# A two-group encoder layer on one core: other buffers for the first sweep's weights, another order of the output projection

## The chip, the cores and the metric

The kernel runs on one core of a Trainium2 chip. The metric is the device time of one execution in microseconds. The core has a TensorE (PE) for matrix products, a VectorE (DVE), a ScalarE (ACT) and a GpSimd (POOL) for elementwise work, and a SyncE (SP) whose queue issues nearly all DMA transfers of this kernel. Each engine takes its own instructions strictly in order; semaphores order them between engines.

## The reference

One encoder layer is applied with the same weights to two groups of tokens: a prompt of 1024 and a sample of 512, each with 16 meta tokens in front. In outline:

```
proj = rmsnorm(x) @ w_in            # 2048 -> 5440 columns, split into 8 parts
y_f   = real(fft2(u_f)) @ w_fmix    # Fourier mixing, 512 wide
y_mla = softmax attention, 8 heads  # low-rank queries, keys and values
y_d   = difference of two softmax attentions, 4 heads, relative bias
y = concat(y_f, y_mla, y_d) * silu(gate)
out = rmsnorm(x + y @ w_o)          # meta tokens dropped
```

All data are float32, and the result must be accurate to float32. Every matrix product is therefore three products of split operands: `hi*hi`, `hi*lo`, `lo*hi`, where `hi` is the rounded value in the PE's fast float32 form and `lo` is the remainder.

## The kernel before, in words

**Splitting.** `split` (lines 97 to 105) makes `hi` with one ACT instruction and `lo` with one DVE instruction that subtracts `hi` from the source. In the profile these are L101 and L102. A weight tile is 128 x 4 x 128 (256 KB); its halves are called `wh` and `wl` and lie in a pool `w` of three buffers, the raw tile `wr` in one of four.

**The weight stream.** `w_order` (line 197) writes down once the order in which all weight tiles are used. `fetch_w` (323) keeps up to three split tiles ready and up to three further entries loaded; `load_w` (272) issues the loads, `prepare_w` (292) splits. The program fixes the order of the PE's instructions alone. On ACT, DVE, POOL and SP the compiler's scheduler orders instructions beforehand, by its own estimate of when each becomes ready; at run time that order stands, also where a transfer takes longer than was estimated.

**Input projection.** `inproj` (378) uses one level of a Strassen-like scheme: the projection of pairs of weight column blocks with halves of the tokens becomes seven sweeps over sums and differences of operands, `b11`, `t1`, `t2`, `t3`, `t4`, `b21`, `b22`. There are 21 pairs in each (`PAIRS`). A sweep takes each pair in two weight entries ("jobs" below), each with 4 weight blocks x 3 products x 2 column ranges (512, and 256 or 264) = 24 matmuls (L374). The first three pairs of `b11` are treated together at the start; the other 18 give 36 jobs of the kind `a11`. Such a job loads two tiles, the block of the second column (`raws[0]`) and that of the first (`raws[1]`). The first is split for the PE. The difference of both, `ws` (one DVE subtraction, L302), goes to DRAM as `s3` (L306), for a later sweep. Both tiles come from one pool, `wq`, whose six buffers go to whichever load is next, as they come free. The loads are issued by line 247. A second's buffer is free after the subtraction, a first's only after its split, and that must wait until PE has released a `wh`/`wl` buffer. In the same sweep the next operand `t1` is built (L404, L430, L431, L102), results go to DRAM (L541 copies, L534 stores), and `bias_vectors` (1199) makes a small table through tiles of the tag `st`, four buffers, which nothing else uses in that sweep.

**Middle.** Up-projections (`upproj`), attention and Fourier mixing of the sample (G2), then of the prompt (G1). Attention has more work for ACT and DVE than for PE; `Chain.merge` therefore puts projection work between its steps, in units of a cost estimate (3 x 512 / 2400 = 0.64 for three 512-wide matmuls). `START[i]` is the amount of projection work put ahead of the first score product of stage i, so that its loads can land; stage 3 is the difference attention of G2. The score product is L1051; L1018 makes its key operand `kd`.

**Output projection.** The 16 row blocks of `y` are treated in four parts (`OUT_PARTS`, line 75), and a last piece (rows 12 to 15 of the prompt). `outproj_parts` (1263) runs beside the prompt's attention: for each of 16 column blocks `d`, the part's matmuls, then one addition per token block that takes the sum so far (`stage`, loaded by L1250 or L1244 or, in the first part, from the input by L1247) and the accumulator (L1295), and a store (L1301). All of these share six `stage` buffers. A sample part of 8 rows has 24 matmuls of 512 columns to an addition; a prompt part of 4 rows has 12, for each of two token blocks. The part that completes the sample also squares and scales (`outproj_scale`, L1256 to L1261). After that, `outproj_end` for G2 runs as a side generator, one step per `d` of the following parts: a load, a multiplication (L1356, on POOL for each third d, otherwise on DVE) and a store (L1357).

**Tail.** The last piece, rows 12 to 15 of the prompt's two token blocks, keeps all results in SBUF. `outproj` (1316) makes, for each d, 12 matmuls for a token block, the addition (L1338) and the squares and scales (L1259 to L1261). Before, the order is: both blocks for d 0 to 7 with the same weight tile; the first block for d 8 to 15, whose seven last tiles stay in an own pool `wt`; then the second block for d 8 to 15 in two column halves. `outproj_end` sums the squares over partitions (L114), takes the power -1/2 on POOL (L118), spreads it to rows (L129, L131) and multiplies 16 result tiles (L1360). The first block's end is advanced once per 0.7 units of the second block's first half:

```
            for gap in end:
                fill.some(0.7)
                if not fill.gens:
                    break
            fill.rest()
            fill = Chain(rows[2:3])
            fill.merge(weave(self.outproj_end(G1, 512, sums[1], sp, pa, (0, 256)), end, 1))
```

Of the kernel before, what the change touches and what calls it, by code (L numbers as in the profile page):

```python
# [74 lines left out]
OUT_PARTS = [(SAMPLE, 0, 8), (SAMPLE, 8, 8), (PROMPT, 0, 4), (PROMPT, 4, 8)]  # L75


class K:
    def __init__(self, tc, ins, outs):
        self.tc = tc  # L80
        self.nc = tc.nc
        self.ins = ins
        self.outs = outs
        self.scr = [{}, {}]
        self.uid = 0
        self.w_tail = 0, None
# [110 lines left out]
    def w_order(self):  # L197
# [43 lines left out]
        for _, e0, n in [*OUT_PARTS, (PROMPT, 12, 4)]:  # L241
            out += [("w", self.ins["wo"][b], k0, 4) for b in range(16) for k0 in range(e0, e0 + n, 4)]
        return out
# [19 lines left out]
    def split_w(self, i, wr, k0, n=4):  # L263
        left, pool = self.w_tail
        if len(self.w_list) - i > left:
            pool = self.wp
# [5 lines left out]
    def load_w(self):  # L272
# [17 lines left out]
        self.w_loaded.append((i, job, [self.raw_w(self.wq, "wq", *x) for x in src]))  # L290
# [908 lines left out]
    def bias_vectors(self, sp, pp):  # L1199
# [5 lines left out]
        def run():  # L1205
# [6 lines left out]
            for c in range(0, NDELTA, 516):  # L1212
# [3 lines left out]
                st = self.t(sp, [P, HALF], "st", bufs=4)[0:DIFF_H, 0:516]  # L1216
# [46 lines left out]
    def outproj_parts(self, yps, ys, sp, pp):  # L1263
# [3 lines left out]
        for ip, (blocks, e0, n) in enumerate(OUT_PARTS):  # L1267
# [14 lines left out]
            for i in range(0, len(todo), len(blocks)):  # L1282
# [24 lines left out]
                next(side, None)  # L1307
# [5 lines left out]
            if ip == 1:  # L1313
# [59 lines left out]
    def run_all(self):  # L1373
# [11 lines left out]
        with ExitStack() as es, ExitStack() as es2:  # L1385
# [14 lines left out]
            self.wq = p1.enter_context(pool("wq", 3, True))  # L1400
            slots = [p1.enter_context(pool("x0", 1, True))]
# [62 lines left out]
            with pool("d1", 2) as ap:  # L1464
                fill.merge(attend(G1, self.diff_ops, ap, 0))
            yf = es2.enter_context(pool("yf", 1))
# [7 lines left out]
            wt = es2.enter_context(pool("wt", 7))  # L1474
            ws = {}


            fill = Chain([self.outproj([(first, y0, sums[0]), (second, y1, sums[1])], range(8), (0, 512), ws, rp, sp, pa)])
            fill.rest()
            self.w_tail = (7, wt)  # L1480
            rows = [self.outproj([(p, y, a)], range(8, 16), cut, ws, rp, sp, pa)
                    for p, y, a, cut in ((first, y0, sums[0], (0, 512)), (second, y1, sums[1], (0, 256)),
                                         (second, y1, sums[1], (256, 256)))]
            Chain(rows[0:1]).rest()
            fill = Chain(rows[1:2])
            end = self.outproj_end(G1, 0, sums[0], sp, pa)
            for gap in end:
                fill.some(0.7)
                if not fill.gens:
                    break  # L1490
            fill.rest()
            fill = Chain(rows[2:3])
            fill.merge(weave(self.outproj_end(G1, 512, sums[1], sp, pa, (0, 256)), end, 1))
            fill.rest()
            drain(end)
# [165 lines left out]
```

## Time and profile before

| | |
|---|---|
| median of three runs | 2954.14 us (2951.81 to 2954.59) |
| the profiled execution's own time | 2959.01 us |
| its span, first to last instruction | 2957.2 us |
| PE busy | 2820.2 us, 95% |
| PE weight loads | 2470.0 us, 84% |
| DVE, ACT, POOL busy | 1776.5, 1148.7, 431.4 us |
| data moved by DMA | 566.51 MB, mean 192 GB/s |

PE is busy nearly everywhere; the busy share counts a matmul from its issue to its end, and matmuls overlap. So the number of matmuls in a stretch, beside the stretch's length, says more than the busy time: where matmuls have the same sizes, fewer of them in the same time are lost time. The granted clock (PEclk) says by how much PE's clock was cut; a cut clock does not show as idle time. A wait names the instruction that waited, what released it, the total, the count and the longest.

### The profile page before, as it was taken

Reading aid. Unit: us, or ns where it says so; the run is one execution under the profiler, and the core shown is the slowest. Engines: PE = TensorE matmul, PEld = TensorE weight load, DVE = VectorE, ACT = ScalarE, POOL = GpSimd, SP = SyncE. Lnnn points to the kernel's source line nnn. Section 1 sums busy time; section 2 is a strip of 40 time slices with the busy share of each in tenths; the row PEclk is TensorE's granted clock in tenths of the full one; section 3 lists DMA queues with packets and bytes.
Section 4 is the critical chain, followed back from the end, with each engine's and each line's share of the span. In section 5 each row is a group of like instructions: output and inputs, shape, how many; then the busy total and the mean of one; then the engine's idle time right before and its main releaser. Section 6 shows DMA issues by size and latency. Waiting matters only on the chain.

```text
span 2957.2 us, 45520 instructions
## 1 busy us (share of the span) xinstructions
PE 2820.2 (95%) x16360; PEld 2470.0 (84%) x16360; DVE 1776.5 (60%) x3263; ACT 1148.7 (39%) x2086; POOL 431.4 (15%) x536
## 2 busy tenths in 40 slices
PE   7889999999999999998899999999999989999986
PEld 6768888888888888886797888889999967888876
DVE  9236355476634445676856645566676649777656
ACT  5223221132322322224644743444555425444443
POOL 4010000011000100101211220222222212222100
PEclk9999999999999999999999999999999999999998
DMA  7668788888855656886555346544344476444254
GB/s 255 198 195 286 226 255 294 276 273 294 287 184 151 203 166 191 248 277 184 172 165 179 122 144 214 181 139 140 119 132 129 132 231 223 141 126 128 77 175 150
DMA packets 331379, 566.51 MB, mean 192 GB/s; under 512 B 50464, under 2 KB 121248, under 8 KB 330978
## 3 DMA queue, kind: packets, MB, share of 16 engines
q1 hardware_dynamic: 330704, 560.28, 59.4%
q0 software_dynamic: 448, 3.32, 0.5%
q8 instruction: 129, 2.11, 0.3%
q14 instruction: 98, 0.80, 0.1%
HBM read 388.39 MB, written 175.05 MB: 191 GB/s over the span
## 4 chain that ended last, share of the span: by engine, by line
PE 78%; DMA 9%; DVE 7%; issue 3%; ACT 2%; SPq 1%; POOL 1%; DVEq 0%; ACTq 0%; POOLq 0%
PE A L374 58%; PE S L962 6%; DMA wq<-in_win_dram 3%; PE T L1116 3%; PE S L1051 2%; PE T L1132 2%; PE T L1131 2%; PE T L1133 2%; DVE wl L102 1%; PE S L820 1%; DMA xr<-in_xt_dram 1%; DMA bt<-bvec 1%; DVE pe L904 1%; DVE ws L302 1%; DVE res L1360 1%
## 5 line engine op out<-in xcount | busy, mean ns | idle before, releaser
L374 PE MATMUL A<-x0h,wl 128*128 128x512 f32 x1376 | 358.4, 342 | 32.2 <-DVE wl L102 32.0
L101 ACT CAST wh<-wr 128x512 fp32r<-128x512 f32 (+1 forms) x342 | 206.2, 603 | 435.9 <-PE A L374 379.7
L374 PE MATMUL A<-x0h,wh 128*128 128x512 f32 x1376 | 359.3, 343 | 7.5 <-ACT x0h L104 7.5
L374 PE MATMUL A<-x0l,wh 128*128 128x512 f32 x1376 | 356.8, 341 | 0.1
L374 PE MATMUL A<-yh,wh 128*128 128x512 f32 (+1 forms) x800 | 328.7, 411 | 28.6 <-DVE stage L1295 19.1
L102 DVE TENSOR_TENSOR wl<-wr,wh 128x512 fp32r<-128x512 f32 (+1 forms) x342 | 245.2, 718 | 149.7 <-ACT wh L101 144.5
L374 PE MATMUL A<-yl,wh 128*128 128x512 f32 (+1 forms) x800 | 312.6, 391 | 1.6 <-DVE yl L102 1.5
L374 PE MATMUL A<-yh,wl 128*128 128x512 f32 (+1 forms) x800 | 312.1, 390 | 0.0
L374 PEld LDWEIGHTS A<-x0h,wl 128*128 128x128 f32 x1376 | 213.4, 190 | 68.4 <-DVE wl L102 38.5
L374 PE MATMUL A<-x1h,wh 128*128 128x512 f32 (+2 forms) x1040 | 269.0, 340 | 0.0
L374 PE MATMUL A<-x1l,wh 128*128 128x512 f32 (+2 forms) x1040 | 267.4, 338 | 0.0
L374 PE MATMUL A<-x1h,wl 128*128 128x512 f32 (+2 forms) x1040 | 266.7, 338 | 0.5 <-DVE wl L102 0.5
L374 PEld LDWEIGHTS A<-x0h,wh 128*128 128x128 f32 x1376 | 213.9, 191 | 39.1 <-ACT x0h L104 7.5
L374 PEld LDWEIGHTS A<-x0l,wh 128*128 128x128 f32 x1376 | 214.7, 190 | 31.4 <-DVE x0l L105 0.6
L101 ACT CAST wh<-ws 128x512 fp32r<-128x512 f32 x132 | 81.6, 620 | 357.6 <-PE A L374 301.4
L374 PEld LDWEIGHTS A<-yh,wh 128*128 128x128 f32 x800 | 154.9, 194 | 50.5 <-DVE stage L1295 15.1
L302 DVE TENSOR_TENSOR ws<-wq,wq 128x512 f32<-128x512 f32 x168 | 122.3, 728 | 115.8 <-DMA wq<-in_win_dram 94.0
L102 DVE TENSOR_TENSOR pl<-T,ph 126x512 fp32r<-126x512 f32 (+1 forms) x240 | 159.5, 685 | 45.3 <-ACT ph L101 43.7
L101 ACT CAST ph<-T 126x512 fp32r<-126x512 f32 (+1 forms) x240 | 132.6, 585 | 129.3 <-PE T L1116 126.6
L374 PEld LDWEIGHTS A<-yh,wl 128*128 128x128 f32 x800 | 154.1, 193 | 32.8
L374 PEld LDWEIGHTS A<-x1l,wh 128*128 128x128 f32 x1040 | 160.8, 189 | 23.1
L374 PEld LDWEIGHTS A<-x1h,wl 128*128 128x128 f32 x1040 | 159.5, 188 | 23.7 <-DVE wl L102 0.8
(211 smaller groups left out, 5712.7 us busy)
## 6 DMA issues: line engine op xcount, KB each, us to landing
wq<-in_win_dram SPq DMA_DIRECT2D x252, 256.0 KB, 4.4
wr<-in_wo_dram SPq DMA_DIRECT2D x128, 256.0 KB, 3.3
wr<-in_win_dram SPq DMA_DIRECT2D x98, 256.0 KB, 3.6
res<-stage SPq DMA_DIRECT2D x96, 256.0 KB, 3.0
stage<-res SPq DMA_DIRECT2D x88, 256.0 KB, 3.4
xr<-in_xt_dram SPq DMA_DIRECT2D x56, 388.0 KB, 5.5
stage<-y SPq DMA_DIRECT2D x48, 256.0 KB, 3.8
wr<-in_wuq_dram SPq DMA_DIRECT2D x48, 192.0 KB, 2.8
```

What stands on the lines that cost most here:

```text
L101: nc.scalar.copy(hi, src)
L102: nc.vector.tensor_tensor(lo, src, hi.bitcast(F32), ALU.subtract)
L302: nc.vector.tensor_tensor(sm, a, c, op)
L374: self.nc.tensor.matmul(ps, ww[:, kk, :], x[k][:, c:c + m], start=(k == 0 and ip == 0), stop=(k == nk - 1 and ip == 2))
L820: nc.tensor.matmul(o, z[:, c, :], tabs[j][:, c, hl, :], start=(c == chunks[0] and ip == 0), stop=(c == chunks[-1] and ip == 2))
L904: ttr(two(dst), src, two(add), 1.0, -3.0e38, ALU.add, ALU.max, accum_out=mx[0])
L962: nc.tensor.matmul(ps[:, c:c + n], qq, k[:, k0:k0 + n], start=(ip == 0), stop=(ip == 4))
L1051: nc.tensor.matmul(ps[:, c:c + n], qq[:, sub, sl], ks[sub][:, k0:k0 + n], start=(ip == 0), stop=(ip == 1))
L1116: nc.tensor.transpose(ps[0:g.kc, c, :], pn[0][:, a:a + g.kc], self.ident)
L1131: nc.tensor.matmul(o, vh[:, c, :], ph[:, c, :], start=(c == 0), stop=False)
L1132: nc.tensor.matmul(o, vh[:, c, :], pl[:, c, :], start=False, stop=False)
L1133: nc.tensor.matmul(o, vl[:, c, :], ph[:, c, :], start=False, stop=False)
```

## The change

It has three parts and a constant.

1. In `a11` jobs the second column's tile goes to a tile of the tag `st` of the pool `s1` (four buffers) in place of `wq`, so that the six buffers of `wq` serve the firsts alone. `bias_vectors` takes its tiles from the tag `u` (seven buffers) instead of `st`.
2. The second and third part of the output projection change places, so that the sample is completed in the third part. Its end runs beside the fourth part, with two steps in each of the first four d.
3. In the tail the first block takes all 16 d alone. The tiles of d 8 to 15 stay in a pool `wt` of eight buffers; those of d 0 to 7 are loaded and split a second time for the second block (eight more entries in the weight stream). The first block's end is advanced once per 1.7 units of the second block's first 8 rows and of the first column half of the others.
4. `START[3]` goes from 6.0 to 11.0.

```diff
-OUT_PARTS = [(SAMPLE, 0, 8), (SAMPLE, 8, 8), (PROMPT, 0, 4), (PROMPT, 4, 8)]
+OUT_PARTS = [(SAMPLE, 0, 8), (PROMPT, 0, 4), (SAMPLE, 8, 8), (PROMPT, 4, 8)]
...
+        out += [("w", self.ins["wo"][b], 12, 4) for b in range(8)]
...
-        left, pool = self.w_tail
-        if len(self.w_list) - i > left:
-            pool = self.wp
+        pool = self.w_kept if 8 < len(self.w_list) - i <= 16 else self.wp
...
-        self.w_loaded.append((i, job, [self.raw_w(self.wq, "wq", *x) for x in src]))
+        raws = [self.raw_w(self.wq, "wq", *x) for x in src[kind == "a11":]]
+        if kind == "a11":
+            raws.insert(0, self.t(self.w_side, [P, HALF], "st", bufs=4)[:, 0:512].rearrange("p (a b) -> p a b", a=4))
+            self.nc.sync.dma_start(raws[0], src[0][0][:, k0:k0 + 4, :])
+        self.w_loaded.append((i, job, raws))
...
-                st = self.t(sp, [P, HALF], "st", bufs=4)[0:DIFF_H, 0:516]
+                st = self.t(sp, [P, HALF], "u", bufs=7)[0:DIFF_H, 0:516]
...
-                next(side, None)
+                for _ in range(1 + (d < 4)):
+                    next(side, None)
...
-            if ip == 1:
+            if final:
                 side = self.outproj_end(G2, 0, (None, ssq), sp, pp)
...
+            self.w_side = s1
...
+            self.w_kept = es2.enter_context(pool("wt", 8))
...
-            wt = es2.enter_context(pool("wt", 7))
...
-            fill = Chain([self.outproj([(first, y0, sums[0]), (second, y1, sums[1])], range(8), (0, 512), ws, rp, sp, pa)])
-            fill.rest()
-            self.w_tail = (7, wt)
-            rows = [self.outproj([(p, y, a)], range(8, 16), cut, ws, rp, sp, pa)
-                    for p, y, a, cut in ((first, y0, sums[0], (0, 512)), (second, y1, sums[1], (0, 256)),
-                                         (second, y1, sums[1], (256, 256)))]
-            Chain(rows[0:1]).rest()
-            fill = Chain(rows[1:2])
+            Chain([self.outproj([(first, y0, sums[0])], range(16), (0, 512), ws, rp, sp, pa)]).rest()
+            for d in range(8):
+                del ws[d]
             end = self.outproj_end(G1, 0, sums[0], sp, pa)
-            for gap in end:
-                fill.some(0.7)
-                if not fill.gens:
-                    break
+            rows = [self.outproj([(second, y1, sums[1])], ds, cut, ws, rp, sp, pa)
+                    for ds, cut in ((range(8), (0, 512)), (range(8, 16), (0, 256)), (range(8, 16), (256, 256)))]
+            fill = Chain(rows[0:2])
+            for _ in end:
+                fill.some(1.7)
             fill.rest()
             fill = Chain(rows[2:3])
-            fill.merge(weave(self.outproj_end(G1, 512, sums[1], sp, pa, (0, 256)), end, 1))
+            fill.merge(self.outproj_end(G1, 512, sums[1], sp, pa, (0, 256)))
             fill.rest()
-            drain(end)
...
-START = (16.0, 15.6, 12.0, 6.0, 12.0, 8.4)
+START = (16.0, 15.6, 12.0, 11.0, 12.0, 8.4)
```

More of the change, by code (lines that the diff above doesn't have):

```diff
@@ L85, in __init__ @@
         self.uid = 0
-        self.w_tail = 0, None
     def nm(self, s):
```

## The prediction

> **What bounds the kernel now.** I read the page first, for the engine shares and the slices.
>
> ```profile
> span 2957.2 us, 45520 instructions
> ...
> PE   7889999999999999998899999999999989999986
> ...
> PEclk9999999999999999999999999999999999999998
> ```
>
> A slice is 74 us. PE is the bound; it is short of work in the first three slices, in two in the middle (near 1350), in one near 2400, and at the end. These are the places of the change. Next the windows, which give a stretch its length, the busy time and count of PE, PEld, DVE, ACT and POOL, then the granted clock, the DMA share and GB/s.
>
> ```profile
> 84.00:240.00 156.00, 131.72 (x686) 108.57 (x685) 49.63 (x64) 35.64 (x72) 12.56 (x6) 0.96 0.61 191
> 240.00:360.00 120.00, 119.48 (x678) 104.34 (x677) 59.60 (x80) 33.46 (x63) 4.32 (x2) 1.00 0.82 264
> 2040.00:2280.00 240.00, 240.00 (x1514) 219.86 (x1513) 159.87 (x341) 128.43 (x232) 64.78 (x88) 1.00 0.41 129
> 2395.00:2460.00 65.00, 49.50 (x217) 40.20 (x216) 40.71 (x77) 22.55 (x38) 9.49 (x11) 0.89 0.87 269
> 2460.00:2814.00 354.00, 336.99 (x1934) 290.05 (x1934) 262.24 (x589) 162.91 (x298) 75.47 (x106) 1.00 0.43 137
> 2834.00:2900.00 66.00, 65.58 (x283) 52.75 (x282) 38.20 (x59) 37.96 (x59) 0.00 (x0) 1.00 0.46 145
> 2900.00:2944.00 44.00, 31.77 (x218) 30.41 (x216) 30.03 (x69) 17.32 (x37) 1.96 (x2) 0.84 0.53 180
> ```
>
> 84 to 240 us is most of the first sweep, 240 to 360 the next, with the same kind of matmuls. The second row runs 678 in 120 us, 0.177 us each. At that rate the first sweep's 686 would take 121.4 us; they took 156. So 34.6 us are lost there: 24.3 idle by the waits below, most of the rest at a cut clock (0.96). The waits of that stretch say on what, the first two lines for PE and DVE, the others for SP's own queue:
>
> ```profile
> DVE ws L302 <- DMA wq<-in_win_dram: 90.9, 22, 6.7
> ...
> PE A L374 <- DVE wl L102: 24.3, 14, 3.8
> ```
>
> ```profile
> SPq L247 <- DVE ws L302: 83.4, 27, 5.3
> ...
> SPq L247 <- DVE wl L102: 7.7, 7, 2.9
> ```
>
> PE waits for a weight's low part on DVE. DVE does that late because its queue has the subtraction `ws` of a later job ahead of it, and that waits for a load. The load was issued late because SP waited for a buffer that an earlier subtraction frees (83.4 us), seldom for one that a split frees (7.7 us). The chain of work shows one turn of this circle, start and duration:
>
> ```profile
> 129.04 0.70 DVE ws L302
> ...
> 129.76 0.33 SPq L247
> ...
> 131.13 5.72 DMA wq<-in_win_dram
> ...
> 136.97 0.70 DVE ws L302
> 137.69 3.15 DMA wq<-in_win_dram
> ...
> 140.92 0.70 DVE ws L302
> ```
>
> Two jobs take 140.92 - 129.04 = 11.88 us, and two transfers lie in line. PE needs 48 x 0.177 = 8.5 us for two jobs. So the circle is the bound of this sweep, not DMA's rate: the next sweep moves 264 GB/s with PE at full rate.
>
> **Part 1, own buffers.** The load at 137.69 starts 0.02 us after the subtraction at 136.97 ends, whose buffer it takes. With four buffers for the seconds, such a load is free of that subtraction and goes out a job or more earlier; the firsts, alone in six buffers, can run up to six jobs ahead of the split. Without the 3.15 us the circle is 8.7 us for two jobs, against PE's 8.5. 686 matmuls are 14.3 such pairs, so 3 us of the 34.6 would remain, a gain of 32. That is one bound. The other comes from what stays: a first's buffer still comes free only after a split, and the scheduler may now put one subtraction between each two splits. Then each job has an issue, a landing, a subtraction and a split in line.
>
> ```profile
> L102 DVE TENSOR_TENSOR wl<-wq,wh 128x512 fp32r<-128x512 f32 x26 | 21.1, 831 | 3.2 <-ACT wh L101 3.2
> ```
>
> With this row's 0.83 us that is 0.33 + landing + 0.70 + 0.83. At a landing of 3.15 us a job takes 5.0 us, at 5.72 us it takes 7.6, against 5.94 now; over the 26 splits of the row that is from -24 to +43 us. The same bytes in less time (191 x 156 / 125 = 238 GB/s) lie between the two window rows. I take -20: nearer to the first bound, since SP's wait for subtractions is eleven times that for splits, but not all of it, since landings will differ from the scheduler's estimate as they do now. The Trainium skill, page "DMA: Bandwidth & Descriptors", section "Latency and other measured facts", speaks against earlier loads: an HBM access takes 0.2 us on average but 2 us at high load, so an estimate by it, 3.15 + 1.8 us to land, would make a job 6.8 us and the sweep 23 us slower. This trace agrees as far as the two landings above go, 3.15 us alone and 5.72 us among others.
>
> The table's tiles in "u" instead of "st" cost nothing: four more tiles pass through seven buffers of which each unit of the sweep takes one. If that cover is gone, a result copy waits for one such transfer once or twice, under 5 us, which is inside the bounds.
>
> **Part 2, order of the parts.** The stage 2395 to 2460 is the passage from one attention to the next. PE has 15.5 idle us there, and DMA is at 0.87, its highest. What moves there, with count and KB, and what PE waits for:
>
> ```profile
> stage<-in_xt_dram SPq DMA_DIRECT2D x12, 256.0 KB, 3.6
> res<-stage SPq DMA_DIRECT2D x12, 256.0 KB, 4.7
> ...
> stage<-res SPq DMA_DIRECT2D x6, 256.0 KB, 5.7
> wr<-in_wo_dram SPq DMA_DIRECT2D x6, 256.0 KB, 4.7
> out_dram<-stage SPq DMA_DIRECT2D x6, 256.0 KB, 4.2
> ```
>
> ```profile
> PE A L374 <- DVE stage L1295: 11.8, 3, 7.0
> ```
>
> These are the prompt's four-row part, with an addition to each 12 matmuls, and the end of G2 beside it. After the change the sample's second half runs here: for the same 144 matmuls 6 loads and 6 stores of sums instead of 24 in all, 12 weights instead of 6, no end of G2 (12 transfers). That is 42 transfers becoming 24, 4.7 MB less, and at 269 GB/s 17.5 us of DMA time; additions that need a `stage` buffer fall from 12 to 6. Against this stand two ACT and one DVE instruction more per d for the sample's squares and scales, off PE's path as long as PE waits for additions. The bounds are -20 (15.5 idle and 5 of the clock, 49.5 x 0.11) and, if squares and scales delay the attention's own steps, +5. I take -10, half of the idle and clock loss, since the attention's loads stay.
>
> What moves out goes to two places. The prompt's four-row part now lies in 2040 to 2280, where PE has 240 of 240 us and DMA 0.41: 16 additions, 32 sums moved and 16 weights fewer are 16 transfers more, 4.2 MB in 240 us; I cost them at nothing, the cover being the attention's gaps, which PE fills; without it each exposed landing is some 4 us. The end of G2 goes into 2460 to 2814.
>
> ```profile
> L1356 DVE TENSOR_TENSOR stage<-stage,rb x11: 678/686/691, 2340.9 to 2537.3; 128x512 f32<-128x512 f32 x11
> ...
> L1356 POOL TENSOR_TENSOR stage<-stage,rb x5: 1281/1299/1681, 2374.5 to 2519.1; 128x512 f32<-128x512 f32 x5
> ```
>
> There DVE is busy 262 of 354 us and PE already idles 17. Eleven multiplications of 0.69 us on DVE and five of 1.30 us on POOL, 14 us of work, lie beside the score chain on the same engines, and each may stand ahead of a step of it while its load lands. Some 4 of the 16 are there already (they end at 2537). So 0 to +10; I take +3. The Trainium skill, page "SBUF — State Buffer", section "Who interferes with whom", says that a DVE instruction with two SBUF inputs contends with a GpSimd instruction that reads SBUF; by it the five on POOL would also hold up DVE, for at most 6.5 us, which the range has.
>
> **The constant.** At the start of stage 3 PE waited once for the first score's keys:
>
> ```profile
> PE S L1051 <- DVE kd L1018: 5.2, 1, 5.2
> ```
>
> Five more units are 5 / 0.64 = 7.8 groups of three 512-wide matmuls. A matmul of that size is 66 / 283 = 0.233 us by the windows row from 2834, so 5.5 us of work cover that wait, if its weights are there: three entries are split ahead, and 7.8 groups need 2.6. It goes from -5 to, if they aren't, 0 (the work is only done earlier). I take -3.
>
> **Part 3, the tail.** What PE waits for from 2814 on, and three of DVE's groups from 2834 on:
>
> ```profile
> PE A L374 <- DVE res L1338: 9.4, 3, 6.3
> ...
> PE T L114 <- DVE ssq L1260: 2.6, 2, 1.4
> PE T L129 <- POOL rc L118: 1.6, 2, 1.1
> ```
>
> ```profile
> L1338 DVE TENSOR_TENSOR res<-stage,A 128x512 f32<-128x512 f32 x24 | 16.5, 686 | 14.6 <-PE A L374 14.6
> L1260 DVE TENSOR_TENSOR ssq<-ssq,tmp 128x512 f32<-128x512 f32 x22 | 15.2, 692 | 9.5 <-ACT tmp L1259 9.1
> ...
> L1360 DVE TENSOR_TENSOR res<-res,rb 128x512 f32<-128x512 f32 x16 | 9.8, 688 | 1.0 <-ACT rb L131 1.0
> ...
> L102 DVE TENSOR_TENSOR wl<-wr,wh 128x512 fp32r<-128x512 f32 x14 | 9.6, 689 | 4.9 <-ACT wh L101 4.9
> ```
>
> From 2900 to 2944 the first block's 16 multiplications stand in DVE's queue ahead of the second block's additions, and PE, out of accumulators, waits 9.4 us; its sum over partitions and rows wait some 2 more (half of 2.6 and 1.6; the other half belongs to the last end, which stays). Afterwards 16 rows of the second block lie beside that end. The clock of 0.84 there costs some 5 us more (31.77 x 0.16). So up to -16. What is added: eight weights, each 256 KB, an ACT cast and a DVE split. PE's work is the same. In the second block's first 8 rows a row is 12 x 0.233 = 2.8 us of PE, and DVE has a split, an addition, a square's sum and 2.56 / 1.7 = 1.5 multiplications, 4.5 x 0.69 = 3.1 us. DVE falls 2.4 us behind there, and may wait for a weight besides. The first block's 16 rows need 3 x 0.69 = 2.1 of 2.8 us. If the order is as unlucky as now, the saved 11 us come back as waits of rows. Bounds -16 and +4; I take -9.
>
> **The sum** for the profiled execution: -20 - 10 + 3 - 3 - 9 = -39 us. It took 2959.0 us, 2957.2 of it span, and the median of the runs is 2954.1; I take the difference from the median: **2915 us**.
>
> **The rivals.** All of the sweep's loss goes: -32 to -36 in place of -20, the sum 2902. For it: 8.7 us against 8.5. Against it: the circle has other queues in it, the stores in SP's.
>
> The sweep gains nothing, since firsts now wait for splits as the seconds did for subtractions: the rest alone, -19, gives 2935. This happens where a landing in the one-for-one order is about 4.1 us (0.33 + 4.1 + 0.70 + 0.83 = 5.94); it is also what follows if the scheduler leaves the loads where they were, that is, if the change does not do what it says.
>
> Slower: the same one-for-one circle with landings above 4.1 us. At 5.72 us it costs 26 x 1.64 = +43 us; with the other -19 the time is 2978. It outweighs the rest from a landing of 4.8 us on (26 x 0.73 = 19). For it: five of six buffers held by firsts that wait for a split is what a longer lead leads to. Against it: a transfer alone in line landed in 3.15 us, and the seconds no longer share those buffers.
>
> **How the numbers follow.** Forecast 0.42, full gain 0.24, no gain in the sweep 0.21, slower 0.13. The range is 2892 to 2950: below it lies full gain with the better bounds of passage and tail (some 0.08), above it most of the slower case (0.12). A measurement of this kernel can tell about 0.2% (6 us) from no change. Faster by more than that: the first three cases but for a tenth of the third and some of the mishaps in the passage and the tail, 0.80; within it 0.07; slower 0.13.
>
> **What would show it.** Right: from 84 us on, matmuls at 0.177 us each, PE's wait for the low part under 10 us, SP's wait for subtractions under 20, the sweep over about 20 us sooner; in the passage after the prompt's first attention PE idle near 8 us and DMA below 0.75; PE's wait for L1338 under 4 us; the multiplications L1360 apart from each other. Wrong: a circle in the chain of work with a load, a subtraction and a split per job; PE waits for L1051 in the last attention growing by over 6 us; a DVE without a gap in the second block's rows with PE waiting for it.

## The result, and the profile after

| | before | after |
|---|---|---|
| median of four runs | 2954.07 us (2951.81 to 2954.59) | 2913.76 us (2912.1 to 2918.23) |
| the profiled execution | 2959.01 us | 2912.1 us |
| its span | 2957.2 us | 2910.2 us |

The ratio after to before is 0.9867, with an interval of 0.9850 to 0.9884: 1.33% or 40.3 us faster, by medians. The two profiled executions differ by 46.9 us, since that of before lies 4.9 us above its median and that of after 1.7 us below. Terms read from the traces therefore add up to more than the medians show.

In the kernel after, lines stand a few further down: the split is L100 and L101 (L101 and L102 before), the load of a second tile L292, the subtraction L305, the matmul L377, the score product L1054, the addition of a part's sum L1298, the sum of squares L1263, the residual addition L1342, the end's multiplication L1364. The page of after, in the lines shown of before:

```profile
span 2910.2 us, 45585 instructions
...
PE   8999999999999999999999999999999989999986
```

Two of the three thin slices at the start are full now, and so are the two in the middle; the passage's slice and the end show as they did. The stages, as windows (length, then busy time and count of PE, PEld, DVE, ACT, POOL, then granted clock, DMA share, GB/s): the first sweep, the difference attention of G2 up to the prompt's MLA attention, its first part alone, and the passage from the prompt's first attention to its second.

```profile
84.00:240.00 156.00, 149.11 (x819) 125.22 (x818) 65.39 (x79) 44.92 (x87) 15.59 (x8) 0.99 0.69 221
1289.10:1905.00 615.90, 592.91 (x3602) 520.05 (x3601) 385.62 (x848) 319.19 (x666) 99.12 (x181) 0.99 0.56 173
1289.10:1439.30 150.20, 139.07 (x803) 119.71 (x802) 111.65 (x232) 85.16 (x180) 19.97 (x37) 0.95 0.60 187
2350.00:2437.20 87.20, 78.65 (x402) 66.39 (x401) 66.85 (x137) 49.64 (x89) 15.42 (x17) 0.96 0.64 195
```

In the first sweep 819 matmuls run in the 156 us that held 686. At the prediction's 0.177 us each they need 145.0 us, so 11.0 us of loss are left of 34.6. By count, a job of 24 matmuls takes 156 x 24 / 819 = 4.6 us on average, against 156 x 24 / 686 = 5.5 before. The last three windows are cut at the same matmuls as these of before:

```profile
1311.80:1938.90 627.10, 597.56 (x3601) 524.71 (x3601) 388.90 (x850) 319.23 (x666) 98.05 (x181) 0.98 0.55 171
1311.80:1472.40 160.60, 141.21 (x802) 121.19 (x802) 119.78 (x245) 87.10 (x185) 22.52 (x39) 0.94 0.58 179
2384.20:2480.90 96.70, 80.55 (x403) 67.44 (x402) 65.77 (x130) 35.71 (x63) 17.18 (x20) 0.93 0.81 255
```

The stretch of 3601 matmuls lost 11.2 us in length and the passage 9.5. What PE waits for in the whole run of after:

```profile
PE S L1054 <- DVE sd L909: 16.3, 14, 6.5
PE A L377 <- DVE wl L101: 8.7, 8, 2.6
PE A L377 <- DVE res L1342: 7.8, 3, 4.2
PE A L377 <- DVE stage L1298: 7.7, 1, 7.7
```

The low part's wait was 24.3 us in 14 places of the first sweep alone (84 to 240 us); there it is now:

```profile
PE A L377 <- DVE wl L101: 5.3, 5, 2.6
```

Of the wait for the addition of a part's sum, the three places of the passage (11.8 us) are gone. The wait for the residual addition, which part 3 was about, went only from 9.4 to 7.8.

Every one of these kernels has 16360 matmuls, so the k-th starts earlier or later by a number that adds up, stage by stage, what was gained so far. In us against the profile of before, for the kernel after and for the four parts alone (experiments below; between places where an experiment runs the code of before, its figures still move by up to 5 us, the difference of one execution from another):

| up to matmul | start before | after | part 1 | constant | part 2 | part 3 |
|---|---|---|---|---|---|---|
| 1200, end of the first sweep | 267.3 | -22.4 | -22.7 | -3.3 | -0.2 | -1.6 |
| 7200, G2's difference attention begins | 1311.8 | -22.6 | -23.0 | -3.6 | +0.1 | -1.9 |
| 11200, the prompt's MLA attention runs | 2004.8 | -35.0 | -25.4 | -14.2 | -1.4 | -6.5 |
| 13600, the passage begins | 2384.2 | -34.2 | -25.4 | -14.2 | -0.1 | -6.5 |
| 14000, its end | 2480.9 | -43.7 | -24.9 | -15.0 | -8.6 | -8.5 |
| 15600, end of the last attention near | 2775.9 | -42.5 | -24.9 | -14.8 | -4.0 | -7.8 |
| 16359, the last | 2945.5 | -47.4 | -26.0 | -15.5 | -5.5 | -12.3 |

### The profile page after: what moved, and what is told of

The parts are those of the page before. It is cut to its first block, busy times and chain, and to the rows that moved or that the text cites. A ratio compares the mean times of both kernels' runs of the same rounds, so it can differ in the third digit from the quotient of the medians.

```text
span 2910.2 us, 45585 instructions
## 1 busy us (share of the span) xinstructions
PE 2807.3 (96%) x16360; PEld 2458.4 (84%) x16360; DVE 1774.6 (61%) x3271; ACT 1152.5 (40%) x2094; POOL 431.7 (15%) x536
## 4 chain that ended last, share of the span: by engine, by line
PE 74%; DMA 7%; DVE 6%; ACT 2%; issue 2%; SPq 1%; POOL 1%; DVEq 0%; ACTq 0%; POOLq 0%
PE A L377 56%; PE S L965 6%; PE T L1119 3%; PE T L1134 2%; PE T L1135 2%; PE T L1136 2%; PE S L1054 2%; DMA raw<-kd 1%; DVE pe L907 1%; DVE wl L101 1%; DVE pe L1069 1%; PE S L823 1%; DMA wr<-in_wo_dram 1%; DMA stage<-res 1%; DMA stage<-y 1%
## 5 line engine op out<-in xcount | busy, mean ns | idle before, releaser
L100 ACT CAST wh<-wr 128x512 fp32r<-128x512 f32 (+1 forms) x350 | 210.9, 603 | 427.3 <-PE A L377 366.6
L377 PE MATMUL A<-x0h,wh 128*128 128x512 f32 x1376 | 358.5, 342 | 9.6 <-ACT x0h L103 7.5
L377 PE MATMUL A<-x0h,wl 128*128 128x512 f32 x1376 | 355.5, 340 | 8.9 <-DVE wl L101 8.7
L377 PE MATMUL A<-x0l,wh 128*128 128x512 f32 x1376 | 355.9, 340 | 3.4 <-DVE x0l L104 3.4
L377 PE MATMUL A<-yh,wh 128*128 128x512 f32 (+1 forms) x800 | 326.0, 408 | 16.0 <-DVE res L1342 7.8
L101 DVE TENSOR_TENSOR wl<-wr,wh 128x512 fp32r<-128x512 f32 (+1 forms) x350 | 252.7, 723 | 134.2 <-ACT wh L100 130.1
L377 PE MATMUL A<-yl,wh 128*128 128x512 f32 (+1 forms) x800 | 310.1, 388 | 0.0
L377 PE MATMUL A<-yh,wl 128*128 128x512 f32 (+1 forms) x800 | 310.1, 388 | 0.0
L377 PE MATMUL A<-x1h,wh 128*128 128x512 f32 (+2 forms) x1040 | 268.7, 339 | 0.0
L377 PE MATMUL A<-x1l,wh 128*128 128x512 f32 (+2 forms) x1040 | 267.1, 338 | 0.0
L377 PE MATMUL A<-x1h,wl 128*128 128x512 f32 (+2 forms) x1040 | 266.3, 337 | 0.0
L377 PEld LDWEIGHTS A<-x0h,wl 128*128 128x128 f32 x1376 | 212.6, 189 | 42.6 <-DVE wl L101 12.4
L377 PEld LDWEIGHTS A<-x0h,wh 128*128 128x128 f32 x1376 | 212.7, 189 | 41.6 <-ACT x0h L103 7.5
L377 PEld LDWEIGHTS A<-x0l,wh 128*128 128x128 f32 x1376 | 214.1, 190 | 35.3 <-DVE x0l L104 4.3
L100 ACT CAST wh<-ws 128x512 fp32r<-128x512 f32 x132 | 81.7, 620 | 363.3 <-PE A L377 306.7
L101 DVE TENSOR_TENSOR pl<-T,ph 126x512 fp32r<-126x512 f32 (+1 forms) x240 | 159.4, 685 | 43.9 <-ACT ph L100 42.8
L377 PEld LDWEIGHTS A<-yh,wh 128*128 128x128 f32 x800 | 152.4, 191 | 37.1 <-DVE stage L1298 8.1
L100 ACT CAST ph<-T 126x512 fp32r<-126x512 f32 (+1 forms) x240 | 132.6, 586 | 128.3 <-PE T L1119 125.7
L377 PEld LDWEIGHTS A<-x1l,wh 128*128 128x128 f32 x1040 | 160.7, 188 | 23.3
L377 PEld LDWEIGHTS A<-yh,wl 128*128 128x128 f32 x800 | 151.8, 190 | 33.0
L377 PEld LDWEIGHTS A<-x1h,wl 128*128 128x128 f32 x1040 | 159.5, 188 | 23.0
L377 PEld LDWEIGHTS A<-x1h,wh 128*128 128x128 f32 x1040 | 159.5, 188 | 22.2
```

What stands on the lines that cost most here:

```text
L100: nc.scalar.copy(hi, src)
L101: nc.vector.tensor_tensor(lo, src, hi.bitcast(F32), ALU.subtract)
L377: self.nc.tensor.matmul(ps, ww[:, kk, :], x[k][:, c:c + m], start=(k == 0 and ip == 0), stop=(k == nk - 1 and ip == 2))
```

## The experiments

### Each part alone

**Part 1 alone.** The hunks of `load_w` and `bias_vectors` and the line that sets `w_side` go into the kernel before.

> The kernel before with part 1 alone (own buffers for the seconds, the table's tiles in the other tag). Theory (a circle of loads and subtractions bounds the first sweep, and the second transfer in line is what goes): PE is ahead by 22 us after the first sweep, as in the trace of after, all later stages as before, the time about 2932 us. Rival (the sweep's gain needs the rest of the change, or the scheduler's other order of later stages takes part of it back): 2940 us or more, or later stages that differ from before by over 5 us.

Measured: 2928.99 us, ratio 0.9926 (0.9914 to 0.9939), 22.5 us less than the 2951.53 of the kernel before beside it. In its trace 819 matmuls lie between 84 and 240 us, as many as in the kernel after; it is 22.7 us ahead at the end of the sweep, and from there on the table moves by under 5 us. The theory holds.

**The constant alone.** `START[3]` goes from 6.0 to 11.0 in the kernel before.

> The kernel before with START[3] = 11 alone. The prediction gave it -3 us; the trace of after is ahead by 10 to 12 us more between 1340 and 1890 us. Theory A (the constant does all of that, by giving the loads of the whole stage more time, not the first wait alone): about -10 us, 2944. Theory B (the constant is worth the first wait, the remainder is a chance of the new order on ACT, DVE and SP that part 1 or 2 brings): -3 to -5 us, 2950.

Measured: 2943.57 us, ratio 0.9977 (0.9967 to 0.9986), 8.0 us less (4.1 to 9.7). That is theory A's number, with an interval that reaches theory B's. In the table its gain lies where the constant acts, 10.6 us between matmuls 7200 and 11200; but 8.9 of them come by matmul 8000, in the stage's first part, so it isn't the loads of the whole stage that gain, as theory A has it. What PE waits for at the start of that stage, before (1311.8 to 1475 us) and with the constant (1308 to 1465):

```profile
PE T L891 <- DVE pl L102: 5.9, 3, 3.1
PE S L1051 <- DVE kd L1018: 5.2, 1, 5.2
PE S L1051 <- DVE sd L904: 4.9, 5, 3.0
```

```profile
PE S L1051 <- DVE sd L904: 6.5, 6, 2.6
PE T L1116 <- DVE pe L1066: 3.5, 2, 1.8
PE A L374 <- ACT wh L101: 3.5, 1, 3.5
...
PE A L374 <- DVE wl L102: 0.3, 1, 0.3
```

The keys' wait of 5.2 us goes, and 3.8 us of waits for weights (the last two lines) take its place, the case in which the projection work put ahead runs out of split weights. But three waits for `pl` (the low part of the transposed probabilities), 5.9 us, go as well. The granted clock in this window is 0.98, against 0.94 in that of before:

```profile
1308.30:1462.00 153.70, 138.74 (x817) 119.77 (x815) 114.73 (x238) 86.15 (x182) 19.87 (x37) 0.98 0.58 185
```

In the kernel after the wait for the keys is gone too and that for `pl` is down to 0.6 us, yet the clock of its window is 0.95. So what the clock adds to the constant's gain isn't settled by these traces.

**Part 2 alone.** The line of `OUT_PARTS` and the two hunks that advance and start the sample's end go into the kernel before.

> The kernel before with part 2 alone (order of the output projection's parts, the end of the sample in the fourth part). Theory (the passage near 2400 us is short of stage buffers and DMA): -10 us in the passage, +2 in the last attention, 2946 us in all, the passage's DMA share under 0.8. Rival (the passage's loss is that of the attention's own loads): under 4 us of gain, 2950 or more.

Measured: 2947.66 us, ratio 0.9988 (0.9979 to 0.9997). By the table 8.5 us are gained in the passage and 4.6 given back in the last attention, and the passage's DMA share is 0.63: the theory's picture, with a time between its number and the rival's. In the passage the only long wait left is the first score product of the next attention:

```profile
PE S L1051 <- DVE sd L906: 8.4, 1, 8.4
```

**Part 3 alone.** The eight more weight entries, the pool `wt` of eight and the new order of the tail go into the kernel before.

> The kernel before with part 3 alone (first block first, eight weights a second time, the end at 1.7 units a step). Theory (11 us of waits go, half of it comes back as DVE falling behind in the second block's rows): -5 us, 2949, with PE's waits for L1338 and its like spread over several rows. Rival (the gain is whole, the trace of after fell short by chance): -9 us or better, 2945.

Measured: 2948.22 us, ratio 0.9991 (0.9982 to 1.0), 3.3 us less, at the edge of what can be told. By the table it gains 4.5 us behind matmul 15600, the kernel after 4.9. PE's wait for the residual addition is 8.6 us in 4 places, one of them 4.2 us long, against 9.4 in 3 before: the theory's number holds, but the waits aren't spread over several rows.

The four single gains are 22.5 + 8.0 + 3.9 + 3.3 = 37.7 us, and the whole change has 40.3 against the 2954.07 beside it, or 37.8 against the 2951.53 of the single parts. So the parts add up within the intervals; none needs another.

### What in part 1 does it

**The ten buffers shared by job.** The four new buffers take both tiles of every other job (those with odd `q`) and the six take both tiles of the rest:

```diff
+        if kind == "a11" and q == 1:
+            raws = [self.t(self.w_side, [P, HALF], "st", bufs=4)[:, 0:512].rearrange("p (a b) -> p a b", a=4) for _ in src]
...
```

> The kernel before with the same four further buffers for the first sweep's loads (and the 0/1 table moved as in the change), but parted by job and not by kind: every other job takes both of its tiles from the four, the jobs between take both from the six. A load then waits for a job 4 or 6 before it, where it waited for one 3 before it; in the change every first waits for a split 6 before it and every second for a subtraction 4 before it. Theory, how many jobs fit into the buffers is what counts: 2928 to 2934 us, like part 1 alone (2929). Rival, it is the parting of firsts from seconds that counts, since a second no longer holds a buffer that a first needs: 2938 to 2946 us, half of the gain or less.

Measured: 2932.01 us, ratio 0.9928 (0.9916 to 0.994), the same as part 1 alone within the intervals; at the end of the sweep its trace is 19.9 us ahead of before, that of part 1 alone 22.7. So most of the gain comes from the number of jobs whose loads can be under way, not from firsts and seconds no longer sharing. One pool of ten for both kinds, or a number between six and ten, wasn't run.

**The kinds exchanged.** Firsts in the four, seconds in the six:

```diff
+        if kind == "a11":
+            raws = [self.raw_w(self.wq, "wq", *src[0])]
+            raws.append(self.t(self.w_side, [P, HALF], "st", bufs=4)[:, 0:512].rearrange("p (a b) -> p a b", a=4))
...
```

> The kernel before with part 1 alone, but the kinds exchanged: the firsts, which wait for a split, take the four buffers, and the seconds, which wait for the subtraction, the six. Theory, both kinds of load stand behind the same job on VectorE, so either may have the four: 2926 to 2933 us. Rival, the firsts' loads are the ones that the circle of the change still goes through, so with four buffers they close it 2 jobs sooner: 2936 to 2944 us.

Measured: 2936.79 us, ratio 0.9946 (0.9933 to 0.9958): a gain of 0.54% where part 1 alone has 0.74%. The rival's range holds it, near its lower end. PE waits 11.4 us for the low part in 8 places between 84 and 240 us where part 1 alone has 4.0 in 3. Most of the loss lies in one stretch, 188 to 216 us, with 109 matmuls where part 1 alone has 142 in the same 28 us: the subtractions, each waiting for a first's load, start at 191.07, 196.75, 202.49 and 207.91, one job to a round trip of 5.6 us. A first holds its buffer until its split, whose cast in turn waits for a weight buffer that PE frees (61.7 us of such waits between 84 and 240 us). That the kind with the longer stay therefore needs more buffers fits these figures; it rests on this one run.

**The subtraction on GpSimd.** What is left in the sweep can be read in the kernel after: DVE's timeline and SP's from 134 to 152 us (start, duration, instruction, and the idle time before it with what ended it).

```profile
134.92 0.69 DVE L305 TENSOR_TENSOR ws<-st,wq 128x512 f32<-128x512 f32 x1 [6.07 <-issue]
135.53 1.28 DVE L101 TENSOR_TENSOR wl<-wq,wh 128x512 fp32r<-128x512 f32 x2
142.05 0.69 DVE L305 TENSOR_TENSOR ws<-st,wq 128x512 f32<-128x512 f32 x1 [5.24 <-DMA wq<-in_win_dram]
143.58 0.69 DVE L305 TENSOR_TENSOR ws<-st,wq 128x512 f32<-128x512 f32 x1 [0.83 <-DMA wq<-in_win_dram]
144.19 0.68 DVE L101 TENSOR_TENSOR wl<-wq,wh 128x512 fp32r<-128x512 f32 x1
150.60 0.69 DVE L305 TENSOR_TENSOR ws<-st,wq 128x512 f32<-128x512 f32 x1 [5.73 <-DMA wq<-in_win_dram]
```

```profile
136.87 0.33 SPq L247 DMA_DIRECT2D wq<-in_win_dram  x1
...
137.83 0.38 SPq L247 DMA_DIRECT2D wq<-in_win_dram  x1
...
145.26 0.38 SPq L247 DMA_DIRECT2D wq<-in_win_dram  x1
```

The splits end at 136.81, firsts' loads go out at 136.87 and 137.83, the subtractions behind them start at 142.05 and 143.58; the next split ends at 144.87, its load goes out at 145.26, the subtraction comes at 150.60. That is the circle that the prediction feared, with a split in it: three jobs in 150.60 - 134.92 = 15.7 us, 5.2 us each, against 5.94 in the turn that the prediction shows of before and 24 x 0.177 = 4.25 that PE needs. Part of it is that a split stands behind a subtraction on DVE that waits for a load. Moved to GpSimd, the subtraction no longer stands there:

```diff
-            nc.vector.tensor_tensor(sm, a, c, op)
+            (nc.gpsimd if kind == "a11" else nc.vector).tensor_tensor(sm, a, c, op)
```

> The kernel after with one edit: the subtraction of the first sweep's jobs runs on GpSimd and not on VectorE, so that a split on VectorE no longer stands behind a subtraction that waits for its second load. Theory, what is left of the sweep's loss after the change (about 12 us between 60 and 240 us) is that standing in line: 2900 to 2906 us, PE's wait for the low part (8.7 us) near 2. Rival, the buffers' number is the limit, or GpSimd's slower subtraction holds the buffers longer and slows VectorE: 2911 to 2922 us.

Measured: 2917.44 us, ratio 0.9885 (0.9871 to 0.9898), not better than the kernel after. At the end of the sweep it is 4 us behind it. The groups of GpSimd (up to 260 us) and of DVE (84 to 260 us):

```profile
L305 POOL TENSOR_TENSOR ws<-st,wq 128x512 f32<-128x512 f32 x36 | 57.0, 1595 | 65.4 <-DMA wq<-in_win_dram 57.0 <-DMA s3uf<-ws 8.4
```

```profile
L101 DVE TENSOR_TENSOR wl<-wq,wh 128x512 fp32r<-128x512 f32 x26 | 26.5, 1030 | 66.3 <-ACT wh L100 66.3
```

The subtraction takes 1.60 us on GpSimd against 0.80 on DVE, and the splits beside it take 1.03 us where they took 0.73. But the loss doesn't lie between 84 and 240 us, where 817 matmuls run, against 819, and PE's wait for the low part is 3.8 us, against 5.3. It lies earlier: by matmul 260, at 63 us, this run is 6.0 us behind the kernel after, and from there to the end of the sweep it makes up 2.0. The stretch from 60 to 84 us, in the kernel after and in this run:

```profile
60.00:84.00 24.00, 22.14 (x114) 18.58 (x113) 21.52 (x23) 9.85 (x18) 6.96 (x3) 0.93 0.73 242
```

```profile
60.00:84.00 24.00, 18.97 (x98) 16.06 (x97) 23.55 (x17) 8.96 (x15) 16.10 (x9) 0.93 0.55 170
```

There DVE is busy for most of the time in both, and in this run it gets through 17 instructions where it got through 23; PE waits 3.7 us at 65 us for a split that took 1.77. So the rival holds at the start of the sweep, where DVE is full, and my theory isn't shown: of the 11.0 us that were left, the move took at most 2.0, and differences of that size lie between executions too. Whether more than ten buffers would take the rest stays open; that wasn't tried.

### How far the constant goes

> The kernel after with the constant of the fourth stage at 16 in place of 11 (6 before). Alone, 6 to 11 brought 8.0 us. Theory, it takes waits out of that stage's first steps, and those are mostly gone at 11: 2910 to 2914 us. Rival, the stage gains by the constant throughout, as much per unit as from 6 to 11: 2903 to 2907 us. Second rival, work put off too long piles up ahead of the attention after it: over 2917 us.

```diff
-START = (16.0, 15.6, 12.0, 11.0, 12.0, 8.4)
+START = (16.0, 15.6, 12.0, 16.0, 12.0, 8.4)
```

Measured: 2909.53 us, ratio 0.9857 (0.9844 to 0.987), 4.2 us less than the kernel after; the intervals overlap. The time lies just below the theory's range and above the rival's.

> The kernel after with the constant of the fourth stage at 24 (11 in the kernel after, 6 before, and 16 gave 2909.5). Theory, the constant takes away waits of that stage's first steps and few are left: 2907 to 2911 us, like 16. Rival, the more work is put ahead the better: 2902 to 2906 us. Second rival, what is put ahead is missing between the later steps of the stage: over 2913 us, with the losses after 1470 us.

```diff
-START = (16.0, 15.6, 12.0, 11.0, 12.0, 8.4)
+START = (16.0, 15.6, 12.0, 24.0, 12.0, 8.4)
```

Measured: 2920.3 us, ratio 0.989 (0.9873 to 0.9907). The same stretch of about 3601 matmuls at 16, then at 24:

```profile
1287.70:1899.00 611.30, 587.63 (x3602) 517.05 (x3601) 387.37 (x850) 318.07 (x666) 100.84 (x181) 1.00 0.56 176
```

```profile
1288.10:1911.10 623.00, 592.90 (x3602) 518.60 (x3601) 384.22 (x849) 319.37 (x666) 99.02 (x181) 0.99 0.55 172
```

With 6 (the kernel before), 11, 16 and 24 the stretch takes 627.1, 615.9, 611.3 and 623.0 us. At 24 the first steps are as good as at 16 (34.0 and 34.6 us ahead of before at matmul 8000), and the loss comes later: at matmul 9600 it is 26.7 us ahead, and 35.4 at 16. The second rival was right by its number and its place. That the work put ahead is missing between later steps, as it says, fits that; it was not shown by a run of its own.

### The tail

What was to be spread in the tail are 16 multiplications of the first block's end. DVE in the kernel after, from 2843 us on, and PE where it stops:

```profile
2843.92 3.10 DVE L1364 TENSOR_TENSOR res<-res,rb 128x512 f32<-128x512 f32 x5 [1.33 <-ACT rb L130]
2846.94 0.68 DVE L1342 TENSOR_TENSOR res<-stage,A 128x512 f32<-128x512 f32 x1
2847.54 3.69 DVE L1364 TENSOR_TENSOR res<-res,rb 128x512 f32<-128x512 f32 x6
2851.15 0.68 DVE L101 TENSOR_TENSOR wl<-wr,wh 128x512 fp32r<-128x512 f32 x1
2851.75 2.49 DVE L1364 TENSOR_TENSOR res<-res,rb 128x512 f32<-128x512 f32 x4
2854.16 0.68 DVE L1342 TENSOR_TENSOR res<-stage,A 128x512 f32<-128x512 f32 x1
```

```profile
2850.40 0.40 PE L377 MATMUL A<-yh,wl 128*128 128x512 f32 x1
2854.98 0.77 PE L377 MATMUL A<-yh,wh 128*128 128x512 f32 x1 [4.19 <-DVE res L1342]
```

All 16 lie within 12.1 us, in bunches of 5, 6, 4 and 1. The residual addition at 2854.16 stands behind ten of them, and PE waits for it. The 1.7 units between them stand in the program text, but only PE's queue keeps the order of the text (`manual_schedule(engines={mybir.EngineType.PE})` in `run`). On DVE the order is the scheduler's, and the multiplications, all ready as soon as `rb` is there, came out as a bunch.

**The first block's scaling on GpSimd.**

```diff
-            eng = nc.gpsimd if d % 3 == 2 and (final or res is None) else nc.vector
+            eng = nc.gpsimd if c0 == 0 and res is not None or d % 3 == 2 and (final or res is None) else nc.vector
```

> The kernel after with one edit in the tail: the sixteen 512-wide multiplications of the first block's scaling run on GpSimd and not on VectorE. In the kernel after they stand in bunches of 5, 6 and 4 on VectorE and TensorE waits 7.8 us for the residual additions behind them. Theory, those bunches are what is left of the tail's loss: TensorE's wait for the residual additions falls to 3 to 4 us, 2908 to 2911 us. Rival, GpSimd's reads slow VectorE while they last (in the run with the subtraction on GpSimd the splits went from 734 to 1030 ns), and the wait only changes its place: 2912 to 2917 us.

Measured: 2906.73 us (four runs, 2906.33 to 2907.49, all below the lowest of the kernel after), ratio 0.9849 (0.9835 to 0.9864). That is below the theory's range. By medians it is 7.0 us less than the kernel after; by ratios, each to the kernel before beside it, 0.18% or 5 us, and the intervals overlap. The trace gives the edit less: of 4.1 us that its tail gains (from 0.9 ahead at matmul 15800 to 5.0 at the last), 2.4 come at matmul 15820, 63 us ahead of the scaling, where PE waits for the last addition of a part's sum (7.7 us in the kernel after, its longest wait, 5.9 here). Behind it 1.7 are left. GpSimd's one line, and DVE beside it:

```profile
2840.92 25.20 POOL L1364 TENSOR_TENSOR res<-res,rb 128x512 f32<-128x512 f32 x16 [2.29 <-ACT rb L130]
```

```profile
2847.80 0.68 DVE L1342 TENSOR_TENSOR res<-stage,A 128x512 f32<-128x512 f32 x1
2848.40 1.19 DVE L101 TENSOR_TENSOR wl<-wr,wh 128x512 fp32r<-128x512 f32 x1
2849.51 1.78 DVE L1263 TENSOR_TENSOR ssq<-ssq,tmp 128x512 f32<-128x512 f32 x1
2851.22 0.67 DVE L1342 TENSOR_TENSOR res<-stage,A 128x512 f32<-128x512 f32 x1
```

DVE is slowed, as the rival has it: the sum of squares takes 1.78 us against 0.69, a split 1.19. But the residual addition, the one instruction that PE waits for, keeps its 0.68 us and comes every 3.4 us. PE's wait for it, 7.8 us in the kernel after, falls less than the theory has it:

```profile
PE A L377 <- DVE res L1342: 5.7, 5, 2.7
```

Of these, 2.2 us lie beside the scaling on GpSimd, where 4.2 lay; the longest, 2.7, comes later, behind twelve 256-wide multiplications of the second block's first half, which are still on DVE.

**With the constant at 16 as well.** Both edits above.

> The kernel after with the constant at 16 and the first block's scaling on GpSimd. If the scaling on GpSimd brings its 3 to 4 us and the parts add up: 2905 to 2908 us, below both kernels. If GpSimd's reads eat the gain: 2909 to 2914 us.

Measured: 2908.89 us, ratio 0.9854 (0.9838 to 0.987): no better than either edit alone, and between the two ranges. Against the kernel after, its trace gains 3.4 us in the constant's stage (6.1 with 16 alone) and 2.7 in the tail (4.1 with the scaling alone), and loses 3.1 between, from matmul 11200 to 15200. Differences of that size lie between executions too: the next run, whose code is that of the kernel after until the tail, loses 3.4 us in the constant's stage. So that GpSimd eats the gain, as the second case has it, isn't shown, and whether 16 is better than 11 stays open.

**The second block's first half on GpSimd too** (constant back at 11):

```diff
-            eng = nc.gpsimd if d % 3 == 2 and (final or res is None) else nc.vector
+            eng = nc.gpsimd if d % 3 == 2 or res is not None and not final else nc.vector
```

> The kernel after with the scaling of the first block and of the second block's first half on GpSimd (16 multiplications of 512 and 16 of 256); the last half's stays as it is. With the first block's alone the time was 2906.7, and there TensorE still waited 2.7 us for a residual addition behind twelve 256-wide multiplications on VectorE. Theory, that wait goes: 2903 to 2905.5 us. Rival, GpSimd slows the additions into the sum of squares, which the last scaling waits for, by as much: 2906 to 2909 us.

Measured: 2903.78 us (five runs, 2903.52 to 2908.15), ratio 0.984 (0.9821 to 0.9859), the fastest of all; every run of it is faster than every run of the kernel after. It lies in the theory's range, and the 2.7 us wait is gone: PE's wait for the residual addition is 3.3 us in 4, the longest 1.2. Behind matmul 15840 its trace gains 3.8 us on the kernel after, against 1.7 with the first block's scaling alone. By time that comparison isn't settled: the intervals overlap. PE's waits for the sum over partitions and for the row of factors went from 2.8 to 5.1 us. The first, 1.7 to 2.5, fits the rival: the 256-wide sums of squares take up to 0.77 us where they took 0.42. The second, 1.1 to 2.6, neither text named: the power that makes the factors is an instruction of GpSimd, and there it stands behind the multiplications.

```profile
2880.72 12.19 POOL L1364 TENSOR_TENSOR res<-res,rb 128x256 f32<-128x256 f32 x16 [1.38 <-ACT rb L130]
2892.88 0.69 POOL L117 TENSOR_TENSOR rc<-rc,mhalf 128x2 f32<-128x2 f32 x1
```

Its input is there at 2891.28, so it starts 1.6 us late. The kernel after itself was run four times, and not again beside these later runs.

## Why the prediction was right, and where it was not

The forecast of 2915 us lies 1.2 us above the median. The sum was right by mechanism in two terms of four, and two errors in size cancelled; that it came so near is luck, since the interval of the measured gain alone is 10 us wide.

**The sweep, -20:** measured -22.4 in the trace and -22.5 for part 1 alone. Both bounds show in the trace: the second's load no longer waits for the subtraction that the next one needs, and the firsts' circle through the split exists, at 5.2 us per job where it is seen, 4.6 on average over the stretch. I named 5.0 us for a landing of 3.15 and 7.6 for one of 5.72; the median landing between 84 and 240 us is 4.2 us for loads into `wq`, which makes 0.33 + 4.2 + 0.70 + 0.83 = 6.1 us a turn; the two turns shown, from subtraction to subtraction, took 7.1 and 7.0. But two jobs can share one round trip, as at 136.87 and 137.83, and three took two turns. The rival "slower" reckoned one turn for each job; that was its error. Of the signs I named, PE's wait for the low part under 10 us was right (5.3). Matmuls at 0.177 us each were not reached (156 / 819 = 0.190). SP's wait for subtractions under 20 us was wrong:

```profile
SPq L292 <- DVE ws L305: 44.9, 17, 5.5
SPq L247 <- DVE wl L101: 16.7, 12, 5.6
```

SP still waits, but for a subtraction four jobs back, so the tile comes in time more often. A queue's wait counts only with what the transfer's reader then waits for. And the run with the ten buffers shared by job points to depth as the cause of most of the gain, where my text laid weight on seconds and firsts having buffers of their own.

**The order, -10 and +3:** -9.5 in the passage (part 2 alone -8.5) and +1.2 in the last attention (alone +4.6). The signs were right: PE idles 87.20 - 78.65 = 8.6 us, I said near 8; DMA's share is 0.64, I said below 0.75. What was not foreseen is the next wait, 6.5 us for the first score product. PE's waits for score products, from the passage to the end of the last attention, grew from 11.3 to 15.6 us, less than the 6 that I named as a sign of being wrong. The prompt's part in the MLA attention cost nothing, as reckoned: from matmul 11200 to 13600 the table moves by 0.8 us.

**The constant, -3, "from -5 to 0":** the term that was mis-sized, and its bound too. Alone it brings 8.0 us. I priced the one wait in the row of the keys; the idle time of the stage's first part fell from 160.60 - 141.21 = 19.4 us to 150.20 - 139.07 = 11.1, and waits for `pl` went as well.

**The tail, -9:** measured -4.9 (part 3 alone -4.5 in the trace, -3.3 by time). The step that failed is that the 1.7 units put the multiplications apart on DVE: they stay in bunches, and PE waits 7.8 us, where I said under 4. The sign of being wrong that I named, a DVE without a gap in the second block's rows with PE waiting for it, is what the lines from 2843.92 on show. The bound that I gave for an order "as unlucky as now" came half true. Running those multiplications on GpSimd gains 1.7 us more by the trace, and 3.8 with those of the second block's first half: part of what was missing.

**The sum:** by the table, -22.4 - 0.2 - 12.4 (matmuls 7200 to 11200) + 0.8 - 9.5 + 1.2 - 4.9 = -47.4, the difference of the two traces; by medians it is -40.3. Of the 12.4 some is no effect of the change: the kernels without the constant move by 1.5 to 4.6 us in that stretch. The forecast's -39 was helped by a constant priced 5 us too low and a tail priced 4 us too high. The gain of the sweep, more than half of the whole, was the term that decided, and it was right.

## What to carry to other kernels

When an in-order queue issues loads into a ring of buffers, ask how many jobs the ring holds and who frees the oldest; a few more buffers, taken from a tag that is idle in that stage, can turn a round trip per job into one for several jobs. Which kind of tile gets more of them can matter: the other way round cost 8 us here. An order written in the program text is an order only on the engines where it is kept: look at the timeline of the engine itself before you count on work being spread there. Before work moves to another engine, look at what stands behind it in that engine's queue, and at how full its neighbour is. A knob that puts work ahead of a stage should be priced by all waits at the stage's start, and tried at further values on both sides: here 24 was worse than 16.

## What the runs showed of the hardware

DVE's instructions beside a busy GpSimd fared differently: those with both operands in SBUF slowed down (the sum of squares from 0.69 to 1.78 us, the split from 0.69 to 1.19), and the residual addition, with one operand in PSUM, did not (0.68). It was the same with 256-wide ones in the last run: the sum of squares went from 0.42 to 0.77 us, the residual addition stayed at 0.41. GpSimd's own multiplication of 128x512 took 1.61 us there. The Trainium skill, page "SBUF — State Buffer", section "Who interferes with whom", gives the rule for it: a DVE instruction with at most one SBUF input does not contend with GpSimd, one with two contends with GpSimd's reads. The trace agrees. It fits that the scaling could be moved, since PE waits there for the addition that has one SBUF input, and that moving the subtraction cost time where DVE was full, since the splits that PE waits for have two.

After the gap of 4.19 us in the tail, the next six matmuls of 512 columns took 2.70 us (2854.98 to 2857.68), 0.45 us each, where 0.233 was the rate before the gap. So that wait cost PE about 1.3 us more than its length.
